# All heads' projections as seven-product pairs, sixteen merge-gate blocks kept plain beside the attention

## The chip, the core and the metric

The kernel runs on one core of a Trainium2 chip. The metric is the device time of one execution in microseconds. The engines are TensorE (PE in the profile, with its weight loads as PEld), VectorE (DVE), ScalarE (ACT), GpSimd (POOL) and SyncE (SP); SP computes nothing here and issues most of the DMAs. Each engine works through its instructions in the order in which they were built.

## The reference, cut to what matters

One step of a hybrid encoder layer for 512 prompt rows and 8 x 16 sample rows, 640 rows in all, of width 2048. What counts here is one wide projection, three kinds of attention on its columns, and gates that are not needed until the end:

```python
h = rms_norm(x, g_pre)
parts = split(h @ w_in)        # 13312 columns = 104 blocks of 128
#  6 stick-breaking heads: q, k, v, gate   24 blocks
#  6 chunk-band heads:     q, k, v, gate   24 blocks
#  4 memory heads:         q, gate          8 blocks
#  3 merge gates of 2048 columns           48 blocks
o_sb = stick_breaking(q, k, v)            # sigmoid, product over a suffix
o_bd = band_attention(q, k, v, rel_bias)  # softmax with a bias
o_mm = memory_attention(q, mk, mv)        # softmax over 256 memory rows
branch = lambda o, g, w: (o * silu(g)) @ w
merged = sigmoid(mg_sb) * branch(o_sb, g_sb, w_up_sb) \
       + sigmoid(mg_bd) * branch(o_bd, g_bd, w_up_band) \
       + sigmoid(mg_mm) * branch(o_mm, g_mm, w_up_mem)
y = x + rms_norm(merged @ w_out, g_post)
```

All arithmetic is fp32. A product of two fp32 operands is made as three matmuls on halves: each operand is split into a high part and a rest (`split`, L113), and high x high, high x rest and rest x high are added up.

## The kernel before, in words

The work goes through five stages, and TensorE is the thread through them.

1. **Prologue**: the memory tokens' K and V, the norm of x, and x as four quarters `b11, b12, b21, b22` (1024 model rows x 320 of the 640 rows each), split, in the right half of the on-chip memory. The first four gate blocks (`FIRST`, L38) are multiplied plainly at its end while the sums of quarters are formed (`sums`, L700).
2. **Pairs** (`block_pair`, L734): two column blocks at once are a 2 x 2 block product, made with seven products in place of eight. A product is 8 x 3 matmuls of 128x128 by 320 columns (L748), so a pair is 168 matmuls. All twelve pairs of the six band heads and the 22 pairs of the other 44 gate blocks go this way. `put_raw` (L808) stores a finished head operand to DRAM (`raw_d`), `put_gate` (L798) a finished gate (`sig_d`). Between pairs SP cuts the cached keys into another layout (`cut_keys`, L820).
3. **Attention** (L840 to L848): sixteen heads in `ORDER` (0 to 5 are stick-breaking, 6 to 11 band, 12 to 15 memory). A block that no pair made is projected plainly by `x_proj` (L189, matmuls on L186): 2 halves x 16 x 3 = 96 matmuls of 320 columns. Stick-breaking heads project q, k, v and gate themselves, four blocks each; memory heads project q and gate, two each; band heads load all theirs from `raw_d` (`loaded`, L371). That makes 32 plain blocks in this stage.
4. **Up-projections** (`up`, L869, matmuls on L186 again): 3 x 16 blocks, first from the stick-breaking heads' results, then memory, then band. The first ones start while the last heads run.
5. **Output projection** in 4 column blocks, norm and residual.

A head's own work: v is transposed (L625), then each of four query blocks goes scores (`mm3`, L171 to L173, tile `s`), sigmoid and running product over VectorE, ScalarE and GpSimd (stick-breaking) or bias and softmax (band, memory), transposes (L458), a split (L114, L115) and the product with v (tile `o`). Beside the prompt's chain run the sample rows' scores (L528) on keys that SP brings and VectorE transposes (L524), and the previous head's sample output (L568 to L596). The tile pools allow one head's `qh, kh, vh` and `wth` at a time.

What sets the order: the program is written head by head, and a scheduler then places the instructions of each engine by its own clock of the program. An instruction that is ready may be placed ahead of one written earlier that waits. `tc.issue_after` keeps the plain projections in line behind one another (L192). Once placed, an engine's order is fixed, and on the chip every instruction waits for the one ahead of it.

Of the kernel before, what the change touches and what calls it, by code (L numbers as in the profile page):

```python
# [8 lines left out]
F32 = mybir.dt.float32  # L9
F32R = mybir.dt.float32r  # L10
AF = mybir.ActivationFunctionType
ALU = mybir.AluOpType
# [4 lines left out]
P = 128  # L17
# [18 lines left out]
LATE = 4  # L36

FIRST = 4  # L38


ORDER = (0, 6, 1, 7, 12, 2, 8, 3, 9, 13, 4, 5, 14, 15, 10, 11)

# [4 lines left out]
def stream_step_kernel(  # L47
# [46 lines left out]

    raw_d = [[dpool.tile([P, NT], F32, name=f"raw_d{n}_{h}") for h in range(6)] for n in range(4)]
    sig_d = [dpool.tile([P, NT], F32, name=f"sig_d{i}") for i in range(3 * KB)]
# [77 lines left out]

    def proj(w, col, kn, src, acc, half=8, back=False):
# [200 lines left out]
    def transposed(col, n, raw):  # L376

        if raw is not None:
            return loaded(n, raw)
        acc = new_acc()  # L380
        x_proj(col, acc)
        t = pa.tile([P, NT], F32, tag=f"l{n}", name=f"l{n}", bufs=2 if n == 0 else 1)
        ACT.copy(halves(t), acc[:, :, :HF])
        return t

    def head_g(col, raw=None):
        sg = stg.tile([P, NT], F32, tag="sig", name="sg")
        if raw is not None:
            SP.dma_start(sg, raw_d[3][raw])
            return sg  # L390
        acc = new_acc()
        x_proj(col, acc)
        ACT.activation(halves(sg), acc[:, :, :HF], AF.Sigmoid)
        DVE.tensor_tensor(halves(sg), acc[:, :, :HF], halves(sg), op=ALU.mult)  # L394
        return sg
# [205 lines left out]
    def causal_head(i):  # L601

        kind, h, c0 = ("sb", i, C_SB) if i < 6 else ("bd", i - 6, C_BD)
        cv = (cache_sb_v, cache_band_v)[i // 6]
        kp, vp, ks, vs = (tokens(t)[:, h] for t in ((sbk_p, sbv_p, sbk_s, sbv_s), (bdk_p, bdv_p, bdk_s, bdv_s))[i // 6])
        strip, strips = None, None
        if kind == "bd":
# [10 lines left out]
            strips = (st[:, TS:], st2)  # L618
        raw = h if kind == "bd" else None
# [30 lines left out]
    def mem_head(h):  # L650
        vn = pa.tile([P, 4, P], F32, tag="nat", name="vnm")[:, :2]
        kn = pa.tile([P, NT], F32, tag="l2", name="knm")[:, :NMEM].rearrange("p (t e) -> p t e", t=2)
        for t, o in ((kn, 0), (vn, 512)):
            SP.dma_start(t, kv_d[:, o + h * P:o + (h + 1) * P].rearrange("(t p) e -> p t e", p=P))
        qt = transposed(C_MM + h * P, 0, None)
        sg = head_g(C_MM + 512 + h * P)
        tp = bank("tp")
# [24 lines left out]

    def gate(i):
        acc = new_acc()
        x_proj(C_GATE + i * P, acc)
# [29 lines left out]
    for i in range(FIRST):  # L715
        gate(i)
        third.append(sums(2 * i))
# [122 lines left out]
    with tc.tile_pool(name="att", bufs=1, reuse_waits="tile") as pa:  # L840
        qm, wTm = zero_padded(4)

        rest = iter(())
        for h in ORDER:
            prompt, score, out = causal_head(h) if h < 12 else mem_head(h - 12)
            interleave(rest, prompt, score)
            rest = out
        interleave(rest)  # L848
    xs.close()
# [8 lines left out]
    def load_o(i):  # L858
        r = po.tile([P, NT], F32, tag="sig", name="or", bufs=5)
        SP.dma_start(r, osg_d[i])  # L860
# [8 lines left out]
    def up(i):  # L869
# [9 lines left out]
        with tc.issue_after(mark if i > 1 else last_mm):  # L879
            proj(w_up[0], j * P, nh, o_src, acc)  # L880
        sig = po.tile([P, NT], F32, tag="sig", name="sig", bufs=5)
        with tc.issue_after(mark):
# [119 lines left out]
```

## Time and profile before

| what | value |
|---|---|
| runs shown | 2084.15, 2087.32, 2087.74 us; median 2087.32 |
| the profiled execution's own time | 2088.03 us |
| its span in the trace | 2086.3 us |
| PE / PEld / DVE busy | 98% / 93% / 53% |
| ACT / POOL busy | 39% / 27% |
| pairs | 136.4 to 974.6 us |
| attention and up-projections | 974.6 to 1858 us |
| output projection and end | 1858 to 2086.3 us |

The profiled execution takes 1.7 us beyond its span, and 0.7 us more than the median. PE's 98% counts a matmul from its issue until its result is out, about 0.31 us for 320 columns, while the next one starts after 0.147 us; so a full PE row can hide some lost time, and what a stage costs is better read from its length and the number of matmuls in it. Rows of a window table give the busy time of each engine with the number of instructions in brackets, then TensorE's granted clock (1 is full speed), the share of the DMA engines and GB/s.

### The profile page before, as it was taken

The numbers are of one execution on the slowest core, as the hardware profiler recorded it, in microseconds if no ns is written. First come the engines' busy times: TensorE is split into PE (matmuls) and PEld (weight loads), VectorE is DVE, ScalarE is ACT, GpSimd is POOL, SyncE is SP. The second block draws the span as 40 slices with busy tenths as digits, with TensorE's granted clock in tenths as the row PEclk, the third lists the DMA queues.
The fourth block names the chain that finished last, engine by engine and source line by source line (L and its number), as shares of the span: only waits on it lengthen the run. The fifth ranks groups of instructions, "written<-read, shape, count | busy, mean of one in ns | idle before, by whom it ended". The sixth has DMA issues, their size and how long they took to land.

```text
span 2086.3 us, 35971 instructions
## 1 busy us (share of the span) xinstructions
PE 2045.1 (98%) x13997; PEld 1934.7 (93%) x13997; DVE 1104.4 (53%) x1804; ACT 817.0 (39%) x1567; POOL 570.1 (27%) x539
## 2 busy tenths in 40 slices
PE   7999999999999999999999999989999999999998
PEld 5999999999999999999999799979998899998886
DVE  6875555555555555555355645555455665542234
ACT  6543444444444444444233333333334232322221
POOL 1155455664444444441010101010100015330000
PEclk9999999999999999999999999989999999999999
DMA  7656665565556655645557646653556875532225
GB/s 264 213 145 157 166 162 146 140 154 147 147 138 162 164 140 136 154 127 167 154 157 214 186 131 197 195 177 109 164 156 216 242 205 172 166 124 72 81 89 214
DMA packets 556889, 336.49 MB, mean 161 GB/s; under 512 B 271761, under 2 KB 507297, under 8 KB 555181
## 3 DMA queue, kind: packets, MB, share of 16 engines
q1 hardware_dynamic: 542942, 294.53, 50.9%
q0 software_dynamic: 6864, 23.93, 3.3%
q10 hardware_dynamic: 6912, 15.73, 2.0%
q8 instruction: 110, 1.80, 0.4%
q14 instruction: 61, 0.50, 0.1%
HBM read 288.75 MB, written 76.35 MB: 175 GB/s over the span
## 4 chain that ended last, share of the span: by engine, by line
PE 91%; DMA 2%; issue 2%; DVE 2%; POOL 1%; ACT 1%; SPq 0%; DVEq 0%; POOLq 0%; ACTq 0%
PE q L748 40%; PE acc L186 32%; PE ya L171 4%; PE ya L172 3%; PE ya L173 3%; PE s L528 2%; POOL merged L888 1%; PE o L587 1%; DMA kc<-keys_d 1%; DMA wr<-in_w_mem_kv_dram 1%; PE tp L458 1%; PE o L171 1%; DMA or<-osg_d 0%; PE o L172 0%; PE o L173 0%
## 5 line engine op out<-in xcount | busy, mean ns | idle before, releaser
L115 DVE TENSOR_TENSOR wl<-wr,wh 128x512 fp32r<-128x512 f32 (+1 forms) x524 | 383.0, 734 | 384.0 <-ACT wh L114 373.3
L114 ACT CAST wh<-wr 128x512 fp32r<-128x512 f32 (+1 forms) x524 | 316.7, 608 | 607.4 <-PE acc L186 250.5
L115 DVE TENSOR_TENSOR wl<-ws,wh 128x512 fp32r<-128x512 f32 x272 | 231.3, 852 | 232.4 <-ACT wh L114 231.8
L748 PE MATMUL q<-xh,wh 128*128 128x320 f32 x1088 | 336.2, 309 | 0.0
L748 PE MATMUL q<-xh,wl 128*128 128x320 f32 x1088 | 336.2, 309 | 0.0
L748 PE MATMUL q<-xl,wh 128*128 128x320 f32 x1088 | 336.1, 309 | 0.0
L114 ACT CAST wh<-ws 128x512 fp32r<-128x512 f32 x272 | 168.9, 622 | 271.3 <-PE q L748 230.3
L186 PE MATMUL acc<-xh,wl 128*128 128x320 f32 x1152 | 269.9, 312 | 0.0
L186 PE MATMUL acc<-xh,wh 128*128 128x320 f32 x1152 | 267.5, 311 | 1.2 <-DVE sg L394 1.2
L186 PE MATMUL acc<-xl,wh 128*128 128x320 f32 x1152 | 267.7, 311 | 0.0
L748 PE MATMUL q<-th,wl 128*128 128x320 f32 x816 | 252.2, 309 | 0.0
L748 PE MATMUL q<-th,wh 128*128 128x320 f32 x816 | 252.1, 309 | 0.0
L748 PE MATMUL q<-tl,wh 128*128 128x320 f32 x816 | 252.1, 309 | 0.0
L748 PEld LDWEIGHTS q<-xh,wl 128*128 128x128 f32 x1088 | 204.6, 188 | 0.0
L748 PEld LDWEIGHTS q<-xl,wh 128*128 128x128 f32 x1088 | 204.5, 188 | 0.0
L748 PEld LDWEIGHTS q<-xh,wh 128*128 128x128 f32 x1088 | 204.5, 188 | 0.0
L186 PEld LDWEIGHTS acc<-xh,wh 128*128 128x128 f32 x1152 | 193.2, 188 | 8.1 <-issue 5.4
L186 PEld LDWEIGHTS acc<-xl,wh 128*128 128x128 f32 x1152 | 193.5, 188 | 7.6 <-issue 7.5
L186 PEld LDWEIGHTS acc<-xh,wl 128*128 128x128 f32 x1152 | 193.9, 188 | 2.3 <-issue 1.8
L741 POOL TENSOR_TENSOR ws<-wr 128x512 f32<-128x512 f32 x102 | 150.7, 1491 | 93.7 <-DVE wl L115 77.1
L748 PEld LDWEIGHTS q<-th,wl 128*128 128x128 f32 x816 | 153.2, 188 | 0.2 <-DVE wl L115 0.2
L748 PEld LDWEIGHTS q<-tl,wh 128*128 128x128 f32 x816 | 153.2, 188 | 0.0
(239 smaller groups left out, 3262.2 us busy)
## 6 DMA issues: line engine op xcount, KB each, us to landing
wr<-in_w_in_dram SPq DMA_DIRECT2D x208, 512.0 KB, 4.7
kc<-keys_d SPq DMA_DIRECT2D x48, 512.0 KB, 5.0
wr<-in_w_out_dram SPq DMA_DIRECT2D x32, 512.0 KB, 3.7
sig_d<-sig ACTq DMA_DIRECT2D x48, 320.0 KB, 5.3
sig<-sig_d SPq DMA_DIRECT2D x48, 320.0 KB, 3.7
keys_d<-in_cache_sb_k_dram SPq DMA_DIRECT2D x96, 128.0 KB, 4.5
keys_d<-in_cache_band_k_dram SPq DMA_DIRECT2D x96, 128.0 KB, 4.5
vc<-in_cache_sb_v_dram SPq DMA_DIRECT2D x48, 256.0 KB, 5.5
```

The costliest lines, as they stand in the source:

```text
L114: ACT.copy(hi, src)
L115: DVE.tensor_tensor(lo, src, hi.bitcast(F32), op=ALU.subtract)
L171: PE.matmul(out, ah, bh, start=start, stop=False)
L172: PE.matmul(out, ah, bl, start=False, stop=False)
L173: PE.matmul(out, al, bh, start=False, stop=stop)
L186: PE.matmul(acc[:, s, :HF], a[:, k], b[s], start=first and f, stop=last and l)
L458: PE.transpose(tp[:, kb * P:(kb + 1) * P], b[:, kb * P:(kb + 1) * P], ident)
L528: return PE.matmul(s[32 * j:32 * j + 32, :nc_], qm[:, j, par * 32:par * 32 + 32], kts[j], start=par == 0, stop=par == 1, tile_position=(0, ...
L587: PE.matmul(o[32 * j:32 * j + 32, :P], l, r, start=i == 0, stop=i == len(steps) - 1, tile_position=(0, 32 * j))
L741: eng.tensor_tensor(o, a[c], b[c], op=op)
L748: PE.matmul(bank_, a[:, k], b[:, k], start=first and k == 0 and n == 0, stop=k == KH - 1 and n == 2, skip_group_check=not first)
L888: POOL.tensor_tensor(merged[:, j], merged[:, j], sig, op=ALU.add)
```

## The change

All 28 pairs of the sixteen heads' operands are now made in the pair stage and stored to DRAM; every head loads all of its operands (`loaded`, `head_g`). Of the 44 gate blocks that the pairs made, 28 stay there and sixteen (`BESIDE`, the gates of the branch that is needed last) are projected plainly during the attention, written as two half-block steps each, 32 steps in all, three per head. `ORDER` now alternates the kinds of heads. The loads of the heads' results and gates in stage 4 have four buffers in place of five.

```diff
-ORDER = (0, 6, 1, 7, 12, 2, 8, 3, 9, 13, 4, 5, 14, 15, 10, 11)
+BESIDE = 16
+PER = 2
+ORDER = (0, 6, 1, 7, 2, 12, 3, 8, 4, 13, 5, 9, 14, 10, 15, 11)
...
-    def x_proj(col, acc):
+    def x_proj_steps(col, acc):
         nonlocal last_mm, back
-        with tc.issue_after(last_mm or last_on(PE)):
-            proj(w_in, col, KB, x_src, acc, back=back)
-        last_mm, back = last_on(PE), False
+        steps, back = proj_steps(w_in, col, KB, x_src, acc, 8, back), False
+        for _ in range(KB // 8):
+            with tc.issue_after(last_mm or last_on(PE)):
+                next(steps)
+            last_mm = last_on(PE)
+            yield
...
     def loaded(n, h):
-        t = pa.tile([P, NT], F32, tag=f"l{n}", name=f"l{n}", bufs=2 if n == 0 else 1)
+        t = pa.tile([P, NT], F32, tag=f"l{n}", name=f"l{n}")
         SP.dma_start(t, raw_d[n][h])
         return t
...
-        sg = head_g(c0 + 2304 + h * P, raw)
-        vt = transposed(c0 + 1536 + h * P, 2, raw)
+        sg = head_g(i)
+        vt = loaded(2, i)
...
-        qt = transposed(c0 + h * P, 0, raw)
-        kt = transposed(c0 + 768 + h * P, 1, raw)
+        qt, kt = loaded(0, i), loaded(1, i)
...
-    pairs = [(C_BD + 768 * n + h * P, put_raw(n, h)) for n in range(4) for h in range(0, 6, 2)]
-    pairs += [(C_GATE + i * P, put_gate(i)) for i in range(FIRST, 3 * KB, 2)]
+    gates = [*range(KB), *range(2 * KB, 3 * KB), *range(KB, 2 * KB)]
+    pairs = [(c + 768 * n + h * P, put_raw(n, i + h)) for c, i in ((C_BD, 6), (C_SB, 0)) for n in range(4) for h in range(0, 6, 2)]
+    pairs += [(C_MM + 512 * n + h * P, put_raw(3 * n, 12 + h)) for n in range(2) for h in range(0, 4, 2)]
+    pairs += [(C_GATE + i * P, put_gate(i)) for i in gates[FIRST:-BESIDE:2]]
...
-        for h in ORDER:
+        left = gates[-BESIDE:]
+        steps = (None for i in left for _ in gate_steps(i))
+        def beside(n):
+            for _ in range(n):
+                yield
+                next(steps, None)
+                yield
+                yield
+        for n, h in enumerate(ORDER):
+            next(steps, None)
             prompt, score, out = causal_head(h) if h < 12 else mem_head(h - 12)
-            interleave(rest, prompt, score)
+            interleave(rest, prompt, score, beside(PER))
             rest = out
+        for _ in steps:
+            pass
```

In the built programs TensorE has 5712 pair matmuls and 3456 plain projection matmuls before (34 x 168 and 36 x 96), and 7056 and 1920 now (42 x 168 and 20 x 96). ScalarE loads its function table 19 times before and 25 times now.

How the plain matmuls (gates and projections on `x`, then up-projections) lie among the heads on TensorE, counted from one head's first transpose (L625 and L659, now L620 and L652) to the next one's. Ahead of the first head stand 219 before and 48 now:

| place in `ORDER` | 1 to 6 | 7 | 8 | 9 | 10 | 11 | 12 | 13 | 14 | 15 | 16 and after |
|---|---|---|---|---|---|---|---|---|---|---|---|
| before | 154 to 403 each | 260 | 220 | 89 | 211 | 208 | 271 | 182 | 163 | 228 | 1145 |
| now | 214 to 236 each | 141 | 44 | 0 | 12 | 0 | 34 | 223 | 214 | 81 | 924 |

TensorE in the middle of a stick-breaking head, between its first query block's transposes and the second one's: before, head 3 (eighth in order; `acc` is a plain projection, `xh` and `xl` the halves of x):

```order
L186 MATMUL acc_15413<-xh01_76,wl_15421 128x320
L593 MATMUL t3_14581<-ident_66,on_14570 128x128
L171 MATMUL s_14585<-kh_14467,qh_14460 128x384
L172 MATMUL s_14585<-kl_14468,qh_14460 128x384
L173 MATMUL s_14585<-kh_14467,ql_14461 128x384
L186 MATMUL acc_15413<-xh00_74,wh_15420 128x320
L186 MATMUL acc_15413<-xh01_76,wh_15420 128x320
L186 MATMUL acc_15413<-xl00_75,wh_15420 128x320
```

The same place now, in head 4 (ninth in order):

```order
L454 MATMUL tp_16333<-ident_66,b_16280 128x128 x4
L589 MATMUL t3_16400<-ident_66,on_16331 128x128
L174 MATMUL s_16404<-kh_16228,qh_16221 128x384
L175 MATMUL s_16404<-kl_16229,qh_16221 128x384
L176 MATMUL s_16404<-kh_16228,ql_16222 128x384
L454 MATMUL tp_16422<-ident_66,b_16408 128x128 x3
L174 MATMUL o_16430<-wth_16272,vh_16217 128x256
L174 MATMUL s_16514<-kh_16228,qh_16221 128x256
```

Where 44 projection matmuls followed the scores of the second query block, the transposes of its result now stand right behind the scores they are made from.

TensorE at the end of head 3 now (seventh in order), where the last gate matmul stands; `oh` and `ol` are the halves of a finished head, and two up-projection blocks are begun:

```order
L189 MATMUL acc_16975<-xh11_80,wl_17161 128x320
L454 MATMUL tp_15637<-ident_66,b_15623 128x128 x2
L174 MATMUL s_15644<-kh_15359,qh_15352 128x256
L175 MATMUL s_15644<-kl_15360,qh_15352 128x256
L176 MATMUL s_15644<-kh_15359,ql_15353 128x256
L524 MATMUL s_15848<-kt_15987,qm4_12705 32x512
L524 MATMUL s_15848<-kt_15851,qm4_12705 32x512
L524 MATMUL s_15848<-kt_15898,qm4_12705 32x512
L524 MATMUL s_15848<-kt_15979,qm4_12705 32x512
L454 MATMUL tp_15662<-ident_66,b_15648 128x128
L189 MATMUL acc_18608<-oh_18574,wh_18611 128x320 x2
L189 MATMUL acc_18658<-oh_18574,wh_18661 128x320 x2
```

Before, the same place in the heads (the seventh and eighth) had projection matmuls throughout, and the up-projections began at the fourteenth head. Now the gates are used up here, and the two up blocks can go no further than the heads that are finished: they need heads 0 to 5, of which 3, 4 and 5 are still to come.

SP around head 5, whose keys are `keys_d5` (before the twelfth, now the eleventh head). Before:

```order
L141 DMA wr_16379<-in_w_in_dram 128x8x128
L141 DMA wr_16437<-in_w_in_dram 128x8x128
L514 DMA kc_16690<-keys_d5_95 128x1024
L514 DMA kc_16759<-keys_d5_95 128x1024
L141 DMA wr_16498<-in_w_in_dram 128x8x128
L514 DMA kc_16807<-keys_d5_95 128x1024
L514 DMA kc_16832<-keys_d5_95 128x1024
```

Now:

```order
L385 DMA l1_17053<-raw_d1_5_144 128x640
L390 DMA sg_16651<-raw_d3_13_176 128x640
L385 DMA l0_17051<-raw_d0_5_128 128x640
L510 DMA kc_17123<-keys_d5_95 128x1024
L510 DMA kc_17230<-keys_d5_95 128x1024
L385 DMA l2_17036<-raw_d2_5_156 128x640
L510 DMA kc_17281<-keys_d5_95 128x1024
L510 DMA kc_17306<-keys_d5_95 128x1024
```

The weights' loads have gone from here, and the head's k, q and v loads stand in the same queue among the key loads.

More of the change, by code (lines that the diff above doesn't have):

```diff
@@ L93, in stream_step_kernel @@
     b12_d = dpool.tile([P, KH, HF], F32, name="b12_d")
-    raw_d = [[dpool.tile([P, NT], F32, name=f"raw_d{n}_{h}") for h in range(6)] for n in range(4)]
+    raw_d = [[dpool.tile([P, NT], F32, name=f"raw_d{n}_{h}") if n in (0, 3) or h < 12 else None for h in range(16)]
+             for n in range(4)]
     sig_d = [dpool.tile([P, NT], F32, name=f"sig_d{i}") for i in range(3 * KB)]
@@ L173, in mm3, with proj_steps @@
         PE.matmul(out, al, bh, start=False, stop=stop)
-    def proj(w, col, kn, src, acc, half=8, back=False):
+    def proj_steps(w, col, kn, src, acc, half=8, back=False):
         starts = range(0, kn, half)
@@ L187, in proj @@
                                   start=first and f, stop=last and l)
-    def x_proj(col, acc):
-        nonlocal last_mm, back
-        with tc.issue_after(last_mm or last_on(PE)):
-            proj(w_in, col, KB, x_src, acc, back=back)
-        last_mm, back = last_on(PE), False
+            yield
+    def proj(*args):
+        for _ in proj_steps(*args):
+            pass
+    def x_proj_steps(col, acc):
+        nonlocal last_mm, back
+        steps, back = proj_steps(w_in, col, KB, x_src, acc, 8, back), False
[4 more added lines that the diff above has]
+            yield
     def x_src(k):
@@ L371, in loaded, with head_g @@
     def loaded(n, h):
-        t = pa.tile([P, NT], F32, tag=f"l{n}", name=f"l{n}", bufs=2 if n == 0 else 1)
+        t = pa.tile([P, NT], F32, tag=f"l{n}", name=f"l{n}")
         SP.dma_start(t, raw_d[n][h])
         return t
[L376 to L394, printed above, removed]
+    def head_g(h):
+        sg = pa.tile([P, NT], F32, tag="sg", name="sg", bufs=2)
+        SP.dma_start(sg, raw_d[3][h])
         return sg
@@ L601, in causal_head @@
     def causal_head(i):
-        kind, h, c0 = ("sb", i, C_SB) if i < 6 else ("bd", i - 6, C_BD)
+        kind, h = ("sb", i) if i < 6 else ("bd", i - 6)
         cv = (cache_sb_v, cache_band_v)[i // 6]
@@ L618, in causal_head @@
             strips = (st[:, TS:], st2)
-        raw = h if kind == "bd" else None
-        sg = head_g(c0 + 2304 + h * P, raw)
-        vt = transposed(c0 + 1536 + h * P, 2, raw)
+        sg = head_g(i)
+        vt = loaded(2, i)
         nat = pa.tile([P, 4, P], F32, tag="nat", name="nat")
@@ L654, in mem_head @@
             SP.dma_start(t, kv_d[:, o + h * P:o + (h + 1) * P].rearrange("(t p) e -> p t e", p=P))
-        qt = transposed(C_MM + h * P, 0, None)
-        sg = head_g(C_MM + 512 + h * P)
+        qt, sg = loaded(0, 12 + h), head_g(12 + h)
         tp = bank("tp")
@@ L681, in put_sig, with gate_steps @@
         ACT.dma_start(sig_d[i], sig)
-    def gate(i):
+    def gate_steps(i):
         acc = new_acc()
-        x_proj(C_GATE + i * P, acc)
+        yield from x_proj_steps(C_GATE + i * P, acc)
         sig = stg.tile([P, NT], F32, tag="sig", name="sig")
@@ L715, in stream_step_kernel @@
     for i in range(FIRST):
-        gate(i)
+        for _ in gate_steps(i):
+            pass
         third.append(sums(2 * i))
@@ L843, in stream_step_kernel @@
         rest = iter(())
-        for h in ORDER:
+        left = gates[-BESIDE:]
[5 more added lines that the diff above has]
+                yield
+                yield
+        for n, h in enumerate(ORDER):
+            next(steps, None)
             prompt, score, out = causal_head(h) if h < 12 else mem_head(h - 12)
-            interleave(rest, prompt, score)
+            interleave(rest, prompt, score, beside(PER))
             rest = out
+        for _ in steps:
+            pass
         interleave(rest)
@@ L858, in load_o @@
     def load_o(i):
-        r = po.tile([P, NT], F32, tag="sig", name="or", bufs=5)
+        r = po.tile([P, NT], F32, tag="sig", name="or", bufs=4)
         SP.dma_start(r, osg_d[i])
@@ L880, in up @@
             proj(w_up[0], j * P, nh, o_src, acc)
-        sig = po.tile([P, NT], F32, tag="sig", name="sig", bufs=5)
+        sig = po.tile([P, NT], F32, tag="sig", name="sig", bufs=4)
         with tc.issue_after(mark):
```

## The prediction

> **What bounds the kernel now.** I read the page first, then windows over the stages, then the plain projections' matmuls alone by window, then the rows of the two places where TensorE is least full. Busy time by engine, from the page:
>
> ```profile
> PE 2045.1 (98%) x13997; PEld 1934.7 (93%) x13997; DVE 1104.4 (53%) x1804; ACT 817.0 (39%) x1567; POOL 570.1 (27%) x539
> ```
>
> TensorE is the bound, but its busy time says little, since matmuls overlap. The windows say more: first the pair stage, then the two thin places in the attention (all engines: PE, PEld, DVE, ACT, POOL, clock, DMA share, GB/s).
>
> ```profile
> 136.40:974.60 838.20, 838.20 (x5715) 837.98 (x5714) 451.36 (x582) 373.61 (x667) 419.14 (x304) 1.00 0.57 147
> 1166.00:1196.00 30.00, 25.57 (x236) 21.70 (x234) 20.17 (x43) 10.88 (x21) 3.00 (x8) 1.00 0.83 244
> 1383.40:1407.00 23.60, 15.05 (x139) 10.94 (x139) 14.81 (x32) 9.05 (x16) 3.09 (x7) 0.77 0.80 243
> ```
>
> The pair stage holds 5712 pair matmuls in 838.2 us: 0.1467 us each, 24.65 us for a pair of 168. TensorE never waits there, and the other engines are at most 54% busy. The thin places are another matter: in 23.6 us only 139 matmuls ran and weight loads took 10.9 us.
>
> The attention with the up-projections, by windows of L186 alone (gates, projections and up blocks; the second number is PE's busy time, its count in brackets):
>
> ```profile
> 974.60:1166.00 191.40, 162.21 (x1056) 155.40 (x1055) 1.00 0.61 179
> 1166.00:1196.00 30.00, 16.31 (x97) 14.38 (x97) 1.00 0.83 244
> 1196.00:1383.40 187.40, 150.03 (x959) 141.63 (x959) 1.00 0.57 168
> 1383.40:1407.00 23.60, 0.39 (x1) 0.35 (x2) 0.77 0.80 243
> 1407.00:1589.00 182.00, 150.39 (x960) 142.74 (x960) 0.99 0.49 140
> 1589.00:1602.00 13.00, 5.32 (x28) 4.27 (x29) 1.00 0.84 273
> 1602.00:1737.00 135.00, 108.94 (x690) 103.31 (x691) 0.99 0.76 225
> 1737.00:1858.00 121.00, 120.52 (x820) 119.89 (x818) 1.00 0.54 158
> ```
>
> 883.4 us hold 4608 such matmuls (the rows' 4611 count some edges twice): 676 us at 0.1467. So sixteen heads' own work and waiting cost 207 us. Window by window, length less count x 0.1467: the four long ones leave 36.5 + 46.7 + 41.2 + 33.8 = 158 us for about 14.3 heads, **11 us for a covered head**; the thin ones leave 15.8, 23.5 and 8.9 us for 0.8, 0.7 and 0.2 of a head. A head costs 11 us where other matmuls fill its waits, and two to three times that where nothing does.
>
> **The change, part by part.** *The products.* 16 plain blocks of 96 matmuls leave the attention and become 8 pairs of 168: 192 matmuls fewer, 28.2 us at 0.1467. The pair stage grows by 8 x 24.65 = 197.2 us; the attention loses 1536 x 0.1467 = 225.3 us. The added pairs cost what the old ones do: in the window above no engine but TensorE is near its limit, the key cutting is over after 33 pairs, and the added stores of q, k, v and gates go where those of the band heads go now.
>
> *What goes with the plain blocks:* copies, sigmoids and products of ScalarE and VectorE that TensorE doesn't wait for. Nothing on the path.
>
> *The cover.* This decides. The table under the change shows that the scheduler spends the sixteen gate blocks at 214 to 236 matmuls per head and is out of them in the seventh head. The up-projections can't take over, since the last stick-breaking head is only the eleventh. So places 8 to 12 (heads 8, 4, 13, 5, 9) run almost bare, then places 13 and 14 are covered again, and half of 15 and the start of 16 are bare. What does a bare head cost? Before has one stretch of it, head 9 from 1383.46 us (VectorE's last two rows belong to the same head):
>
> ```profile
> 1383.46 0.60 PE L625 MATMUL t<-ident,l 128*128 128x128 f32 x4
> 1388.36 0.48 PE L171 MATMUL s<-kh,qh 128*128 128x512 f32 x1
> 1397.06 1.12 PE L458 MATMUL tp<-ident,b 128*128 128x128 f32 x4
> 1398.04 0.67 PE L171 MATMUL s<-kh,qh 128*128 128x384 f32 x1
> 1402.60 0.52 PE L458 MATMUL tp<-ident,b 128*128 128x128 f32 x3 [3.25 <-DVE b L483]
> 1404.07 0.41 PE L171 MATMUL s<-kh,qh 128*128 128x256 f32 x1
> 1405.35 0.41 PE L172 MATMUL o<-wtl,vh 128*128 128x256 f32 x1
> 1408.61 0.35 DVE L483 TENSOR_SCALAR b<-b,sm 128x256 f32<-128x256 f32 x1
> 1413.03 0.28 DVE L452 SCALAR_TENSOR_TENSOR b<-s,strip 128x128 f32<-128x128 f32 x1
> 1415.20 0.28 DVE L483 TENSOR_SCALAR b<-b,sm 128x128 f32<-128x128 f32 x1
> ```
>
> 4.9 us to the first scores, 8.7 until their probabilities are transposed, then 1.0, 4.6 and 1.5 to the third scores at 1404.07. From there 4.9 to the third block's probabilities; the fourth's took 2.5 from bias to end, and I add some 2 for transposes, split and product. Together 30 us. Head 7, at the other thin place, agrees: its scores run from 1165.6 to 1195 with only 37 plain matmuls (5.4 us) between. I take **30 us for a bare band head**. A bare stick-breaking head is not in the trace; the steps of its first query block are, in head 3:
>
> ```profile
> 1346.94 0.40 PE L171 MATMUL s<-kh,qh 128*128 128x512 f32 x1
> 1348.40 0.59 ACT L446 ACTIVATE e<-s 128x512 f32<-128x512 f32 x1
> 1349.06 0.29 POOL L448 TENSOR_SCALAR_AFFINE_SELECT e<-e 128x128 f32<-128x128 f32 x1 [0.18 <-ACT e L446]
> 1349.38 1.23 DVE L471 TENSOR_TENSOR_SCAN e<-e 128x512 f32<-128x512 f32 x1 [2.86 <-POOL e L448]
> 1350.64 0.69 DVE L473 TENSOR_TENSOR b<-b,e 128x511 f32<-128x511 f32 x1
> 1351.60 0.66 PE L458 MATMUL tp<-ident,b 128*128 128x128 f32 x4
> ```
>
> 4.7 us against 8.7. So between 20 us (all four blocks without disturbance) and 30; I take **25**, and for a memory head, whose four blocks have half the columns, **20** (bounds 15 and 28).
>
> *The sum.* Places 8 to 12, less what up blocks fit in (44, 12 and 34 matmuls: 6.5, 1.8, 5.0 us): 23.5 + 25 + 18.2 + 25 + 25 = 116.7. The bare half of place 15 gets 10 and the start of place 16, 18. The other 9.9 heads at 11 make 109. At the stage's start 48 matmuls (7.0 us) must cover the first head's loads, which are issued as the pair stage's buffers come free:
>
> ```profile
> l<-raw_d SPq DMA_DIRECT2D x18, 320.0 KB, 4.2
> 1392.13 1.28 ACT L481 ACT_TABLE_LOAD   x1 [3.01 <-DVE sm L478]
> 1393.42 0.72 ACT L481 ACTIVATE b<-b,sm 128x512 f32<-128x512 f32 x1
> ```
>
> A load (first row, from the DMA issues) lands after 4.2 us, so I put 2 us there (0 to 6). Own cost of the heads now: 116.7 + 28 + 109 + 2 = 256 us, against 207: 49 us more. With the 28 us saved the kernel is 21 us slower: 2088.0 + 21 = 2109 for the profiled execution, which stood 0.7 above the median, so **2108.3 us**. Everything outside (prologue, up blocks at 0.1467, output projection) is unchanged; four buffers in place of five for the up stage's loads cost nothing while a block takes 36 x 0.1467 = 5.3 us and a 320 KB load 4.2.
>
> Six function table loads are added, 1.29 us each from start to the next instruction (the other two rows, ScalarE's in head 9): none in the sum, for the 30 us hold one already; at most 6 x 1.29 = 8 us if all lie on the path. [...]
>
> **The rivals.** *Bare heads run at their undisturbed pace* (faster). Half of the 30 us are waits that cross from one chain to another, such as the scores at 1388.36 to the transposes at 1397.06; if placed for a bare TensorE, they may fall away. The heads would then cost 24, 20 and 16 us and the two part heads 8 and 14: 90.7 + 22 = about 113 in place of 145 (116.7 + 28), so 32 us less and the kernel 11 us faster: 2076. For it: in the thin places DVE is busy only 63 to 67%. Against it: DMA is at 80 to 83% there, and the loads of q, k and v for ten more heads come on top. The point that decides is the mean bare head: at 30/25/20 I have +21, at about 4 us less zero, below that a gain. Chance 0.20; near zero, within 4 us, 0.11. (4 us is 0.2% of the time, about what a measurement of this kernel can tell from no change.)
>
> *The clock falls for the whole bare stretch* (slower still). In head 9's stretch the granted clock is 0.77 and a 256-column matmul starts every 0.21 us; in head 7's it stays 1.00 and the same takes 0.12:
>
> ```profile
> 1405.56 0.41 PE L173 MATMUL o<-wth,vl 128*128 128x256 f32 x1
> 1192.48 0.28 PE L171 MATMUL o<-wth,vh 128*128 128x256 f32 x1
> 1192.60 0.29 PE L172 MATMUL o<-wtl,vh 128*128 128x256 f32 x1
> ```
>
> Some 30 such matmuls and a dozen transposes stand in a head's chain, so half clock all through adds some 4 us to each of six bare heads: +24, 2132. For it: five bare heads follow one another, with no run of plain matmuls between them at which the clock could recover. Against it: my 30 us already hold a part of it. Chance 0.12. [...]
>
> *The change doesn't do what it says.* The few words speak of 32 blocks; the code has sixteen, in 32 half-block steps, and the matmul counts (1920 = 20 x 96) confirm it. With 32 there would be no product saved. Excluded.
>
> **How the numbers follow.** My forecast, slower by 4 to 35 us, has 0.57, the clock's case 0.12: slower 0.69. Within 4 us 0.11, faster 0.20. The forecast's own range, from bare heads 3 us shorter to 2 us longer and all table loads on the path, is 2091 to 2128. The range reaches to the undisturbed pace below and the fallen clock above, and leaves out their outer halves: 2076 to 2132.
>
> **What would show it.** In the changed kernel the pair stage should end at about 136 + 42 x 24.65 = 1172 us; the first seven heads take about 7 x (225 x 0.1467 + 11) = 308 us; then five heads should follow in about 130 us with few plain matmuls, PE's weight loads around half busy there, and the last gate matmul should lie some 150 us ahead of the first full run of up blocks. I am wrong if heads 4 and 5 take under 21 us from first transpose to the next head's, or if the pairs take more than 24.7 us, or if the scheduler's gaps are filled by work I have not counted.

## The result, and the profile after

The changed kernel takes 2157.5 us (median of 2155.90, 2156.26, 2158.76 and 2158.85), against 2087.5 for the kernel before in the same comparison: a ratio of 1.0335 (95% interval 1.0315 to 1.0354). It is slower, as forecast, but by 70 us in place of 21, and above the range (2076 to 2132).

The engines and TensorE's granted clock in 40 slices of the span, from the page of the changed kernel (0.969 of full speed on average, 0.994 before):

```profile
PE 2053.5 (95%) x13805; PEld 1928.3 (90%) x13805; DVE 1166.6 (54%) x1866; ACT 852.7 (40%) x1631; POOL 706.1 (33%) x645
PEclk9999999999999999999999999999678989999999
```

PE's 98% has become 95%, and four of the 40 slices (54 us each) have a clock of 0.6 to 0.8. By windows over all engines: the pair stage, then heads 8, 4, 13, 5 and 9 (places 8 to 12), each from its first transpose to the next head's:

```profile
137.70:1172.40 1034.70, 1034.70 (x7056) 1034.48 (x7055) 563.33 (x718) 449.33 (x804) 552.44 (x409) 1.00 0.53 141
1485.70:1526.10 40.40, 26.46 (x200) 20.11 (x201) 25.65 (x55) 9.99 (x25) 3.98 (x11) 0.79 0.72 209
1526.10:1553.10 27.00, 16.76 (x145) 12.50 (x144) 15.66 (x30) 10.86 (x27) 6.23 (x17) 0.75 0.69 195
1553.10:1578.60 25.50, 14.52 (x123) 10.74 (x123) 13.81 (x40) 8.77 (x22) 0.58 (x1) 0.67 0.54 166
1578.60:1607.50 28.90, 17.35 (x101) 10.94 (x99) 17.83 (x31) 9.93 (x25) 5.95 (x17) 0.71 0.74 214
1607.50:1645.10 37.60, 26.07 (x189) 20.09 (x190) 25.33 (x57) 11.42 (x28) 3.98 (x11) 0.68 0.92 292
```

The pairs end at 1172.4 us, where the forecast had 1172, at 0.1467 us a matmul. All five heads are bare, and no engine has its fill in them: summed over the five, TensorE is busy for 101 of 159 us and VectorE for 98. The plain matmuls alone, in the first seven heads, those five, and the rest up to the end of the up blocks:

```profile
1172.40:1485.70 313.30, 242.60 (x1540) 227.80 (x1540) 1.00 0.74 224
1485.70:1645.10 159.40, 20.16 (x90) 17.27 (x90) 0.72 0.74 220
1645.10:1926.20 281.10, 220.45 (x1442) 214.55 (x1442) 0.95 0.62 181
```

753.8 us hold 3072 plain matmuls, 450.7 us at 0.1467. The heads' own cost is 303 us: 207 before, 256 forecast. Stretch by stretch, against the forecast: 87.4 us (79) for the first seven heads and the start; 159.4 less the 13.2 of 90 matmuls, 146.2 (116.7), for the five; 23.3 (22) for places 13 and 14, 17 (15.5) for place 15, 29 (22.4) for place 16. So 29.5 of the 47 us that are missing lie in the five bare heads.

What "bare" means in a row: TensorE's groups in those five heads, then in the covered heads of the same kernel (1180 to 1480 us). Columns: busy us and mean ns of one, then idle us before them and what ended it. `acc<-oh` are up matmuls, `acc<-xh` gate matmuls.

```profile
L524 PE MATMUL s<-kt,qm 128*32 128x512 f32 x56 | 11.0, 867 | 5.1 <-DVE kt L520 2.6 <-ACT e L541 1.9 <-ACT e L477 0.6
L454 PE MATMUL tp<-ident,b 128*128 128x128 f32 x40 | 10.9, 390 | 22.8 <-DVE b L469 11.4 <-DVE b L479 11.2
L174 PE MATMUL o<-wth,vh 128*128 128x256 f32 x25 | 10.9, 436 | 3.3 <-ACT wth L117 3.3
L189 PE MATMUL acc<-oh,wh 128*128 128x320 f32 x28 | 8.0, 390 | 6.1 <-ACT oh L117 6.1
```

```profile
L524 PE MATMUL s<-kt,qm 128*32 128x512 f32 x96 | 20.1, 604 | 0.3 <-DVE kt L520 0.3
L454 PE MATMUL tp<-ident,b 128*128 128x128 f32 x59 | 10.6, 279 | 1.3 <-DVE b L479 0.7 <-ACT on L586 0.6
L174 PE MATMUL o<-wth,vh 128*128 128x256 f32 x34 | 9.6, 283 | 0.0
L189 PE MATMUL acc<-xh,wh 128*128 128x320 f32 x496 | 116.9, 313 | 0.0
```

The transposes of the probabilities wait for VectorE in both. In the five bare heads TensorE stands idle for it, 22.8 us over 40 transposes; in the covered ones it multiplies gates meanwhile, and 1.3 us are left over 59. The matmuls themselves take 1.4 to 1.5 times as long in the bare heads. Before a gate matmul TensorE does not wait at all (0.0 us over 496); before the up matmuls it waits for their operand (6.1 us over 28).

One wait was not in the prediction. The chain of waits in head 8 (start, duration; `or` and `oh` belong to the up blocks begun for finished heads):

```profile
1515.55 4.60 DMA or<-osg_d
...
1520.17 0.73 ACT oh L117
...
1520.95 0.86 PE acc L189 x4
1521.81 2.12 PE acc L189 x8
1523.93 0.23 PE tp L454
```

A finished head is read back from DRAM, split on ScalarE and multiplied in TensorE's line ahead of head 8's own transposes, which wait for all of it.

### The profile page after: what moved, and what is told of

Its sections match the earlier page's. It is cut to its first block, busy times and chain, and to the rows that moved or that the text cites. A ratio compares the mean times of both kernels' runs of the same rounds, so it can differ in the third digit from the quotient of the medians.

```text
span 2153.8 us, 36053 instructions
## 1 busy us (share of the span) xinstructions
PE 2053.5 (95%) x13805; PEld 1928.3 (90%) x13805; DVE 1166.6 (54%) x1866; ACT 852.7 (40%) x1631; POOL 706.1 (33%) x645
## 4 chain that ended last, share of the span: by engine, by line
PE 89%; DMA 4%; DVE 3%; ACT 1%; issue 1%; SPq 0%; POOL 0%; DVEq 0%; ACTq 0%; POOLq 0%
PE q L742 48%; PE acc L189 22%; PE ya L175 3%; PE ya L174 3%; PE ya L176 3%; DMA kc<-keys_d 2%; PE s L524 2%; PE o L583 1%; DMA or<-osg_d 1%; DVE kt L520 1%; PE tp L454 1%; PE acc L175 1%; PE acc L176 1%; PE acc L174 0%; PE o L175 0%
## 5 line engine op out<-in xcount | busy, mean ns | idle before, releaser
L118 DVE TENSOR_TENSOR wl<-wr,wh 128x512 fp32r<-128x512 f32 x508 | 379.2, 751 | 333.1 <-ACT wh L117 329.9
L117 ACT CAST wh<-wr 128x512 fp32r<-128x512 f32 x508 | 306.2, 608 | 561.2 <-PE q L742 222.4
L742 PE MATMUL q<-xh,wh 128*128 128x320 f32 x1344 | 416.0, 309 | 0.0
L742 PE MATMUL q<-xl,wh 128*128 128x320 f32 x1344 | 415.9, 309 | 0.0
L742 PEld LDWEIGHTS q<-th,wh 128*128 128x128 f32 x1008 | 189.4, 188 | 0.0
L782 POOL TENSOR_TENSOR ws<-wr,ws 128x512 f32<-128x512 f32 x84 | 110.6, 1317 | 195.4 <-DVE wl L118 193.4
L189 PE MATMUL acc<-xh,wh 128*128 128x320 f32 x640 | 149.7, 312 | 0.0
L189 PE MATMUL acc<-xl,wh 128*128 128x320 f32 x640 | 149.3, 312 | 0.0
L189 PE MATMUL acc<-xh,wl 128*128 128x320 f32 x640 | 149.2, 311 | 0.0
L735 POOL TENSOR_TENSOR ws<-ws,wr 128x512 f32<-128x512 f32 x84 | 130.1, 1569 | 23.7 <-DVE wl L118 23.6
```

The source lines that it names most:

```text
L117: ACT.copy(hi, src)
L118: DVE.tensor_tensor(lo, src, hi.bitcast(F32), op=ALU.subtract)
L189: PE.matmul(acc[:, s, :HF], a[:, k], b[s], start=first and f, stop=last and l)
L735: eng.tensor_tensor(o, a[c], b[c], op=op)
L742: PE.matmul(bank_, a[:, k], b[:, k], start=first and k == 0 and n == 0, stop=k == KH - 1 and n == 2, skip_group_check=not first)
L782: POOL.tensor_tensor(b, a, b, op=ALU.subtract)
```

## The experiments

Theory A: the loss is the lost cover; each head without some 200 plain matmuls beside it costs about 19 us more than one with them. Theory B: the loads and the order cost it, cover or not. Theory C: the up blocks begun among the bare heads. Later D (key loads), E1 and E2 (waits or slow matmuls) and F1 to F3 ask what makes a bare head as long as it is. Times of the kernel before lay between 2086.7 and 2088.2 in each comparison.

### More gate blocks beside: 32, 24

```diff
-BESIDE = 16
-PER = 2
+BESIDE = 32
+PER = 4
```

> 32 gate blocks beside the attention in place of sixteen, five half-block steps per head: 34 pairs and 36 plain blocks as in the kernel before, so no matmul is saved; the heads still load everything and stand in the new order, at 240 plain matmuls per head up to the twelfth. Theory A: every head but the end of the fifteenth is covered, so the total is that of the kernel before or a little under, 2072 to 2092. Theory B: 2110 or more, since loads and order are those of the changed kernel.

Measured: **2061.0 us**, ratio 0.9876 (0.9861 to 0.9891): 96 us below the changed kernel and 26 below the one before, though no product is saved against before. B falls: all loads of heads and the new order are in it. The five heads, all engines and then the plain matmuls alone:

```profile
1306.90:1537.50 230.60, 229.96 (x1848) 216.43 (x1847) 118.76 (x240) 99.34 (x194) 19.12 (x51) 1.00 0.67 203
1306.90:1537.50 230.60, 188.06 (x1201) 177.44 (x1200) 1.00 0.67 203
```

1200 matmuls are 176.0 us; the heads' own cost is 54.6 us, 11 each, against 146.2. TensorE is busy for 229.96 of the 230.6 us, and the clock is 1.00.

With `BESIDE = 24` and `PER = 3`:

> Four pairs become eight plain gate blocks beside the attention (24 in all, three per head), the order of the heads unchanged. 203 to 242 gate matmuls per head now reach to the tenth place; places 11 and 12 keep 68 and 20 plain matmuls. Cost in TensorE work: 8 x 96 x 0.1467 - 4 x 24.65 = +14.1 us. Theory A (a head without cover costs what it waits): places 8, 9 and 10 cost 84.6 us now beyond their plain matmuls and should cost 33, so 14.1 - 51.6 = -37.5 us, 2120 (2110 to 2130). Theory B (the heads' own loads and the order of kinds cost, cover or not): only the +14.1 shows, 2172. If the stored heads' up blocks are the main cost (theory C), they still stand in places 11 and 12 and little goes: about 2160.

Measured: **2104.5**, ratio 1.0076 (1.0061 to 1.0091), 16 us below A's 2120 and outside its range. Places 8, 9 and 10 (48.7, 43.3 and 38.7 us, with 230, 224 and 212 plain matmuls) cost 15.0 + 10.4 + 7.6 = 33 us of their own, as A said; place 12 gained 6 us that were not counted, the rest is spread.

### Where the cover stands

The sixteen gate blocks in halves of 48 matmuls, each held behind the matmul written before it, so that they last for eleven heads:

```diff
-            with tc.issue_after(last_mm or last_on(PE)):
+            with tc.issue_after(last_on(PE) if paced else last_mm or last_on(PE)):
...
-    back = True
+    back = paced = True
```

> The same sixteen gate blocks, but each half-block step is held behind the instruction of TensorE that was written just before it, so they lie at 144 matmuls per head over eleven heads and not at 225 over seven. No product, load or head is changed. Theory A (lost cover: a head without plain matmuls beside it costs 25 to 40 us of TensorE's time, a covered one 11): heads 1 to 11 cost 144 x 0.1467 + about 12 us each, only the twelfth is bare, total about 2100 us (2088 to 2115). Theory B (what the change adds to every head, the loads from DRAM and the alternating order, costs the time): 2140 us or more.

Measured: **2206.5**, ratio 1.0575 (1.0553 to 1.0596), 106 us above what A gave. Taken alone this fits B (2140 or more), which the run with 32 blocks excludes. Then the same in groups of 12, one after each step of the head's code:

```diff
-PER = 2
+PER = 11
...
-        for _ in range(KB // 8):
-            with tc.issue_after(last_mm or last_on(PE)):
+        for _ in range(KB // 2 if fine else KB // 8):
+            with tc.issue_after(last_on(PE) if fine else last_mm or last_on(PE)):
...
```

> The sixteen gate blocks of the changed kernel spread over eleven heads, 144 matmuls each, in twelves: after each step of the head's code one group of 12, held behind the matmul written before it. Theory A by amount (a covered head needs some 220 matmuls, each hides its part wherever it stands): 144 hide two thirds of 19 us, 11 x 12.7 = 139 us, against 7 x 19 = 133 hidden now, so the same time within 10: 2147 to 2165. Theory A by place (a matmul hides a wait only where it stands in it, and one that stands elsewhere delays the chain): groups placed by hand in line lose as those of 48 did, 2180 to 2210.

Measured: **2165.3**, ratio 1.0358 (1.0341 to 1.0375), 41 us less for the same matmuls in smaller groups, and at the upper edge of what A by amount gave. The run with 48s from place 2 into place 13 as one window, then heads 1 and 2 (stick-breaking), 12 (memory) and 8 (band) of the run with 12s:

```profile
1225.00:1725.00 500.00, 408.99 (x3162) 369.70 (x3162) 253.40 (x519) 176.99 (x381) 47.12 (x126) 0.88 0.65 194
```

```profile
1268.40:1303.80 35.40, 31.77 (x280) 29.53 (x279) 20.94 (x34) 14.19 (x34) 6.89 (x19) 1.00 0.74 218
1348.60:1383.70 35.10, 31.41 (x280) 29.55 (x279) 19.20 (x34) 14.13 (x34) 6.04 (x15) 1.00 0.74 218
1383.70:1417.30 33.60, 24.37 (x202) 21.81 (x201) 14.46 (x40) 13.28 (x27) 0.58 (x1) 0.85 0.47 143
1465.20:1510.40 45.20, 35.81 (x296) 32.00 (x295) 24.33 (x54) 18.10 (x34) 3.13 (x8) 0.92 0.69 198
```

With 48s, TensorE still stood idle 91 of 500 us. With 12s, a stick-breaking head with 144 gate matmuls (21.1 us) takes 35 us, 6 to 8 more than a bare one below (26.7 and 29.0), so 13 to 15 us of its waits are hidden. The band head with as many keeps 24 us of its own (34.8 bare), and the memory head with 84 keeps 21 (23.9 bare). So cover counts by its amount and by where it stands: in clumps of 48 it leaves more waits open. Whether clumps also delay the head's own matmuls was not shown.

### The order of the heads

All stick-breaking heads by the eighth place, so that their up blocks can be the cover:

```diff
+ORDER = (0, 1, 12, 2, 3, 13, 4, 5, 6, 14, 7, 15, 8, 9, 10, 11)
```

> Only the order of the heads is changed: 0, 1, 12, 2, 3, 13, 4, 5, 6, 14, 7, 15, 8, 9, 10, 11. The gates are still used up after seven heads, but the stick-breaking heads are finished after eight, so the up-projections can cover from the tenth head. Theory A: two bare heads in the middle and parts of three at the end in place of five and two parts, about 2100 us (2085 to 2120). Theory B: no change from 2157 beyond 10 us.

Measured: **2143.2**, ratio 1.0271 (1.0254 to 1.0288), between the theories: 14 us won of 57. A had counted the up blocks as ready cover. From place 8 to their end TensorE waited 22 us ahead of up matmuls for their operand, which has to be read back and split, and the last head cost 44 us of its own.

The order of before in the changed kernel, `ORDER = (0, 6, 1, 7, 12, 2, 8, 3, 9, 13, 4, 5, 14, 15, 10, 11)`:

> The changed kernel with the order of heads of before. The gates again last for seven heads; places 8 to 13 (heads 3, 9, 13, 4, 5, 14) have 0 to 36 plain matmuls, places 14 to 16 are covered. Theory A, from bare heads as measured (stick-breaking 27, band 35, memory 24 us): 27 + 35 + 24 + 27 + 28 + 24 = 165 us and 33 for the three covered ones, 198 against 216 us for places 8 to 16 of the changed kernel: 2140 (2130 to 2155). If the new order itself were what costs, the time would fall back by far more, to about 2110, the forecast of the prediction.

Measured: **2142.7**, ratio 1.0272 (1.0254 to 1.0291). A's working holds to 3 us: six heads are bare, but the last three are covered. So the new order accounts for some 14 of the 70 us; with 32 blocks beside, where it leaves little bare, it costs nothing that shows.

With more gate blocks and all memory heads early as well, so that the up blocks of both kinds cover the last band heads (26 and 28 blocks, `PER = 3`):

```diff
+ORDER = (0, 6, 1, 12, 2, 13, 3, 14, 4, 15, 5, 7, 8, 9, 10, 11)
```

> 26 gate blocks beside (three pairs' worth fewer than with 32: 3 x 24.65 more and 6 x 96 x 0.1467 less, -10.6 us), three per head, and an order in which all stick-breaking and memory heads come before the last five band heads, so that the up blocks of both can stand beside those: 204 to 260 plain matmuls in each of places 1 to 15, only place 12 with 160. Theory A: every head covered, so the kernel with 32 blocks less 10.6 us: 2050 (2042 to 2062). Rival: 210 matmuls cover less than 240 do, or five band heads in a row, whose loads of bias and keys then follow one another, wait for them: 2 us for each of sixteen heads, 2080 or more.

> 28 gate blocks beside, three per head, in the order with the last five heads all of the band kind: 194 to 249 plain matmuls in each of places 1 to 15, and 347 beside the last head. Theory A: against the same with 26 blocks 3.5 us more for the products, about 12 less at place 12 and 13 less at the last head, which had 160 and 136 plain matmuls there: 2061 (2053 to 2070). If what that kernel lost lies in the five band heads in a row and not in the cover, it stays at 2080 or more.

Measured: **2082.7** (0.9973, 0.9961 to 0.9984) and **2071.7** (0.9931, 0.9914 to 0.9948). With 26 the forecast was 33 us too low, and the time is the one that the rival gave. But the rival's band heads in a row (8, 9 and 10) cost 15.5, 13.1 and 11.5 us of their own, as covered ones do. Head 7 at place 12, with 160 matmuls, cost 23, and the last head had 136 beside it, for which I had not allowed. With 28 both have more (own cost 14 and 16 us), and 11 of the 22 us came. What did not come lies in head 8 at place 13, where the gates now end: 24.4 us of its own in spite of 194 plain matmuls, for TensorE stood idle 10 us ahead of the first up matmuls, until their operand was read back and split:

```profile
1570.51 1.43 PE L189 MATMUL acc<-oh,wh 128*128 128x320 f32 x4 [10.32 <-ACT oh L117]
```

And with 30 blocks, four per head, `ORDER = (0, 6, 1, 12, 2, 7, 3, 13, 4, 14, 5, 8, 15, 9, 10, 11)`:

> 30 gate blocks beside, four per head, with the memory heads at places 4, 8, 10 and 13: 240 plain matmuls in places 1 to 11, then 192, 207, 251, 232, and 270 beside the last head. Theory A: all covered, so the kernel with 32 blocks (2061) less 3.5 us for a pair gained and up to 3 us more at places 12 and 13: 2058 to 2064. Rival as with 28.

Measured: **2063.4** (0.9893, 0.9875 to 0.9910), as A gave, no better than 32 in the change's own order.

### The up blocks among the bare heads

Reading back and splitting the stick-breaking results is held until the twelfth head is written:

```diff
-        SP.dma_start(r, osg_d[i])
...
-        split(hh, ll, r)
+        with tc.issue_after(held[0]), tc.issue_after(held[1]), tc.issue_after(held[2]):
+            SP.dma_start(r, osg_d[i])
+            split(hh, ll, r)
```

> The loads and splits of the stick-breaking heads' results for the up-projections are held until the twelfth head is written, so no up work stands among the bare heads. Theory C (the bare heads take 159 us in place of my 130 because TensorE, ScalarE and VectorE wait in line for a finished head's way through DRAM and back, some 5 us at each of three places): the bare stretch falls to about 140 us even without the up work's own 13 us, total 2140 to 2150. Theory A alone (a bare head simply is that long): 90 up matmuls leave waits that they filled, total 2155 to 2170.

Measured: **2150.1**, ratio 1.0303 (1.0288 to 1.0319), 7 us less. C gave about 140 us for the bare stretch, A alone a kernel of 2155 or more; it lies between them. The five heads now hold nothing but their own work:

```profile
1485.40:1520.20 34.80, 20.52 (x156) 13.91 (x157) 23.66 (x52) 9.25 (x24) 3.93 (x11) 0.69 0.78 233
1520.20:1546.90 26.70, 17.12 (x144) 12.92 (x143) 15.19 (x30) 11.14 (x27) 6.54 (x17) 0.69 0.70 196
1546.90:1570.80 23.90, 13.70 (x111) 8.80 (x111) 13.66 (x40) 8.26 (x21) 0.58 (x1) 0.57 0.52 165
1570.80:1599.80 29.00, 18.29 (x101) 11.34 (x99) 17.16 (x30) 10.19 (x26) 6.26 (x17) 0.62 0.86 258
1599.80:1632.60 32.80, 17.79 (x156) 12.91 (x157) 20.40 (x48) 8.09 (x21) 3.93 (x11) 0.76 0.83 247
1485.40:1632.60 147.20, 87.43 (x661) 59.87 (x662) 90.07 (x196) 46.93 (x117) 21.23 (x56) 0.67 0.75 223
```

The last row is all five together. 147.2 us against 159.4: the 90 up matmuls (13.2 us) had added nearly their whole length (12.2 us), not filled waits. Some of that moves: the first up matmuls now wait in place 13, whose own cost rises from 6.9 to 14.4 us.

### What makes a bare head that long

All five runs start from the kernel with the held loads (2150.1, five bare heads 147.2 us). Half of the key loads left out, in every head:

```diff
-                kc = load_k(4 * par + j)
+                kc = kc if j else load_k(4 * par)
```

> The kernel with the up blocks' first loads held back, and in it half of the cached keys left out: each head makes two of its four key loads and transposes the same two tiles twice, so the sample rows' scores are of the wrong keys; instructions on VectorE and TensorE stay the same. Theory D (key loads of 512 KB through two buffers, each waiting for VectorE's transposes of the one before, set a bare head's length): the two band heads go from 34.8 and 32.8 to about 28, the two stick-breaking ones from 26.7 and 29.0 to 24, together some 18 us less than that kernel's 2150: 2132 (2124 to 2140). Theory E (the prompt's chain at a low clock sets the length, the keys only fill its waits): within 5 us of 2150.

Only the first of the three products in the bare heads' scores and outputs (`thin` is set at places 8 to 12):

```diff
     def mm3(out, ah, al, bh, bl, start, stop):
+        if thin:
+            PE.matmul(out, ah, bh, start=start, stop=stop)
+            return
```

> The kernel with the up blocks' first loads held back, and in the five bare heads only high x high of the three products in scores and outputs, so those results lack the rests' parts; VectorE, ScalarE, GpSimd and all DMAs keep their work. A band or stick-breaking head loses 8 score matmuls of 512 to 256 columns and 12 of 256 columns, the memory head 8 of 256 and 4 of 512. Theory E2 (slow matmuls stand in the bare head's chain): at 0.21 us for 256 columns, as the rows of bare heads show, 4 x 5 + 3 = some 23 us less than that kernel's 2150: 2127 (2122 to 2135). Theory E1 (the waits on the other engines and the loads set the length, and the matmuls fit into them): within 5 us of 2150. At full clock (0.12 us) the same matmuls would be worth 13 us at most, 2137.

And both edits together:

> Half of the key loads and two thirds of the bare heads' score and output matmuls left out together. Alone they took 3 and 5 us. F2 (side by side): together more than their sum, 15 to 25 us, 2125 to 2135. F1 and F3: about the sum, 8 us, 2142 (2137 to 2147).

Measured: **2147.1** (1.0281, 1.0265 to 1.0297), **2145.6** (1.0282, 1.0262 to 1.0303) and together **2143.3** (1.0266, 1.0251 to 1.0281): 3, 5 and 7 us, little beside the 7 us by which executions of one of these kernels differ. D and E2 fall, and F2's 15 to 25 us for both together did not come. Without half of the keys the chain of waits in the five heads has 3% of key loads in it in place of 17%, but other lines take their place, and the five heads take 149.6 us.

Then one chain at a time, the prompt's alone and the sample rows' alone (`only_store` stores the head without the sample rows' part):

```diff
+            if 7 <= n <= 11:
+                score, out = iter(()), only_store(heads_sg[-1], h)
```

> The kernel with the up blocks' first loads held back; in the five bare heads the sample rows' scores and outputs are left out (key and value loads of the caches, their transposes, softmax or product, and the output of the sample rows; the store of the head stays). Left is the prompt's chain and the head's own loads. If the prompt's chain sets the length (F1): within 6 us of 2150. If two chains of equal length stand side by side (F2): likewise within 10 us. If they take turns on VectorE, ScalarE and TensorE's lines and so add up (F3): the heads fall to the pace that the prediction gave for undisturbed ones, 24, 20, 16, 20, 24 = 104 in place of 147, 2107 (2095 to 2118).

```diff
+            if 7 <= n <= 11:
+                prompt = iter(())
```

> The complement: in the five bare heads the prompt's four query blocks are left out, and the loads, the transposes of v, the splits, and all of the sample rows' work stay. F1 (the prompt's chain is the length): the heads fall to what the splits and loads take, some 15 us each, 2150 - 70 = 2080. F2 (two equal chains side by side): within 10 us of 2150. F3 (they add up): the part that the prompt does not take, 2150 - 60 to 80 = 2070 to 2090; F1 and F3 part at the run with the prompt alone.

Measured: **2119.2** (1.0151, 1.0134 to 1.0167) and **2100.2** (1.0062, 1.0047 to 1.0077). The five heads with the prompt alone, then with the sample rows alone:

```profile
1487.03:1510.58 23.55, 12.41 (x120) 9.76 (x120) 14.71 (x33) 8.75 (x23) 3.54 (x10) 0.79 0.64 174
1510.58:1535.91 25.33, 12.52 (x48) 9.72 (x47) 10.90 (x19) 7.71 (x18) 5.67 (x16) 0.56 0.32 94
1535.91:1553.88 17.97, 7.34 (x29) 5.53 (x29) 8.18 (x28) 7.50 (x19) 0.56 (x1) 0.51 0.23 74
1553.88:1578.85 24.97, 12.69 (x48) 9.84 (x47) 12.21 (x21) 8.17 (x20) 6.30 (x18) 0.64 0.36 102
1578.85:1605.53 26.68, 13.81 (x64) 9.88 (x64) 14.69 (x34) 7.90 (x19) 3.08 (x8) 0.63 0.71 215
```

```profile
1486.30:1499.65 13.35, 11.40 (x108) 7.45 (x109) 10.11 (x19) 2.65 (x8) 2.68 (x6) 0.55 0.87 281
1499.65:1517.32 17.67, 8.47 (x104) 5.94 (x103) 9.40 (x21) 7.79 (x15) 2.37 (x4) 0.71 0.99 280
1517.32:1533.58 16.26, 7.00 (x90) 4.79 (x89) 6.22 (x13) 3.10 (x10) 1.01 (x2) 0.76 1.04 312
1533.58:1544.03 10.45, 6.78 (x52) 3.54 (x52) 6.57 (x16) 5.48 (x12) 2.94 (x5) 0.50 0.99 331
1544.03:1567.95 23.92, 10.27 (x107) 6.69 (x104) 12.32 (x20) 5.19 (x14) 2.82 (x6) 0.53 1.01 300
```

Alone the prompt takes 118.5 us and the sample rows 81.7; together 147.2, neither the longer one (F1, F2) nor the sum of 200 (all of F3). The 81.7 is too low, for part of what the sample rows cost shows only behind them: at place 13 the own cost of head 14 rises from 14.4 to 31.9 us, with the DMA share at 1.02. With that their chain is nearer 99 us (an estimate), and the finding is the same. The prompt's chain is four fifths of a bare head, and the other chain stretches it by a quarter (28.7 us).

The rows show where that quarter appears. TensorE's idle time (length less PE busy) is 59.7 us with the prompt alone and 59.8 with both: the sample rows' matmuls fill some of the prompt's waits, but their own waits stand in the same line, and on balance the stretch grows by TensorE's busy time (58.8 to 87.4). This is no proof that TensorE's line is where the chains collide: with two of the three products left out its busy time fell by 13.6 us (to 73.9) and the five heads by 3.4. VectorE's and ScalarE's lines hold both chains too, and which one decides stays open.

## Why the prediction was wrong in size

**Right**: the mechanism and its place. The pairs cost 24.6 us each. The gates ended in the seventh head, places 8 to 12 ran bare, and the loss is the cover: with 240 matmuls per head it is gone and turns into a gain. A covered head's 11 us held in a kernel not yet seen (54.6 / 5).

**The step that failed** is the sum for places 8 to 12: "23.5 + 25 + 18.2 + 25 + 25 = 116.7". It measured 146.2, and both parts of it were too small.

- *The price of a bare head*, 30/25/20/25/30 = 130, measured 147.2 without up blocks: 34.8, 26.7, 23.9, 29.0 and 32.8, 7 to 20% more each. I had added up the steps of the prompt's chain. For the band heads, priced from a real stretch, the price held a part of the other chain (30; 23.5 and 26.7 measured with the prompt alone). For the stick-breaking heads 25 was the middle between two bounds; that it is just the prompt alone (25.3 and 25.0) is luck. And head 7 of the kernel before does not support the 30: between 1166 and 1196 us it had 97 plain matmuls, as the row says, 14.2 us, and not 37. The sample rows' chain adds 28.7 us in all, and the price had room for 11.5 of them. This is 17 of the 29.5 us. The rival of the undisturbed pace, 24, 20, 16, 20 and 24 = 104, is not reached even with no sample rows (118.5).
- *"Less what up blocks fit in"*, 13.3 us. An up matmul of a head that has only just been finished hangs on that head's way to DRAM, back and through the split; here it filled no wait but made one. Holding them back shortened the five heads by 12.2 us. A gate matmul's weights are loaded and split too, but nothing in it depends on a head, and TensorE did not wait for it (0.0 us ahead of 496 gate matmuls, 6.1 ahead of 28 up matmuls); the two were taken for the same thing. Up blocks whose operands have been read back in time do cover: places 13 and 14 of the changed kernel have 437 of them and cost 23.3 us of their own.

The other 18 us lie at the start and in the first seven heads (8; the seventh alone, with 141 plain matmuls, cost 15.1) and at places 13 to 16, above all the last (29 against 22.4). No run took those apart; the six table loads that the sum left out may be among them.

**The clock's rival** (2132): the clock did fall in the bare stretch, to a mean of 0.72, and of 0.67 without the up blocks. By itself it does not explain the 17 us: with the prompt alone it was lower still, 0.63 over the five heads, and they took 118.5 us, less than the forecast's 130. Nor do the prompt's slow matmuls: 92 of them left out were worth 5 us, where 23 were expected if they all stood in the chain. What the low clock costs by itself was not isolated. In the traces of the kernels before and after, each record of the granted clock is 0.5 or 1.0 (12 and 36 records), and the mean of 0.72 is 0.5 for 88.7 of the 159.4 us.

**What cover is worth**: with 240 gate matmuls each, TensorE is busy for 229.96 of the five heads' 230.6 us, so the 54.6 us are about the time of their own matmuls in line, and everything else of a head hides. The 87.4 us of PE time in the bare heads would be 58.6 if it went with the clock (an estimate: 87.4 x 0.67), not far from that. So each of the eight pairs between the kernels with 16 and 32 blocks saves 28.2 / 8 = 3.5 us of products and lays bare (96.5 + 28.2) / 8 = 15.6 us of waits.

## What to carry to other kernels

Work that saves matmuls elsewhere can still be worth more as cover (here 15.6 us of waits a pair against 3.5 us of products): count for each latency-bound stretch (one that waits on chains of small steps) how many ready matmuls it needs (here some 200 to 240 per head), and move work out of it only above that number. Cover must be ready when the wait comes; work whose operand has only just been finished and must first be read back and split can add its length in place of filling a wait (here 12.2 us for 13.2 us of up matmuls). And price a bare stretch by all the chains that stand in its in-order engines, not by the longest one (here 147.2 us with both chains, 118.5 with the longer one alone).

## Not expected of the hardware

- In four of the five heads in which only the sample rows' work was left, the DMA share was 0.99 to 1.04 at 280 to 331 GB/s, so the loads look like the limit there; the full bare heads show 0.52 to 0.86.
- In the run with groups of 12 the clock fell with TensorE busy for 73% of a head (24.4 of 33.6 us: 0.85) and stayed at 1.00 with 90% (31.8 of 35.4).
